# Attention in a one-layer encoder: two heads' probabilities turned in 32x32 blocks through DRAM, scores over 64 rows two heads at once, and a new order of the mixer

## The chip, the cores and the metric

One Trainium2 chip, one of its cores. The metric is the device time of one execution in microseconds (us). A core has five engines, each with its own list of instructions: TensorE (PE, matmuls; its weight loads are shown apart as PEld), VectorE (DVE), ScalarE (ACT), GpSimd (POOL) and SyncE (SP, which here only starts DMA transfers). Engines wait for each other through semaphores. PE writes to PSUM, eight banks of 128 x 512 f32; DVE and ACT read PSUM and read and write SBUF.

## The reference

One layer of an encoder on 512 positions with 1024 channels, all float32: a gated feed-forward half-step (2752 wide), a mixer, a second feed-forward half-step, a final norm. The mixer is what matters here:

```python
h = rms_norm(x, mix_norm); u = h @ w_in            # 512 Fourier | q 8x64 | k 2x64 | v 2x64
f_out = fourier_mixer(u[..., :512], fnet_w, fnet_b)
# attention, 8 query heads, 2 key heads (4 query heads share one), heads of 64:
q = rope(rms_norm(q, q_norm)); k = rope(rms_norm(k, k_norm))
scores = q @ k.T * 64**-0.5
p = softmax(scores)                                # over 512 keys
a_out = p @ v
x = x + concat([f_out, a_out]) @ w_out
```

## The kernel before, in words

Channels lie on the partitions and positions along the free axis. Products keep float32 accuracy by splitting each operand into a rounded high part and a low rest (`.h` and `.l` below, the rest by `lows`, one subtraction on DVE) and adding three of the four products: high x high, high x low, low x high.

The feed-forward halves run from the start to about 331 us and from about 485 us to the end. Neither is touched. Between them stands the mixer, written as some 660 small named operations. A string `ORDER` lists their names; `manual_schedule` emits them in that order, so that on each of the five engines the instructions stand, and run, in the order of the list. PSUM banks are handed out by `bank_for` and come back with `read`, also in list order: an operation that takes a bank waits until the last reader of the bank's former tile is done.

The attention runs over four pairs of heads, t = 0 to 3. In a pair, head b = 0 uses the first key head and b = 1 the second; their 64 channels are the lower and the upper 64 partitions. For each chunk c of 128 queries or kc of 128 keys there are these operations (t, b, c stand in the names as digits):

- `q{t}.0` to `.7`, `k.0` to `.7`, `v.0` to `.7`: projections, three matmuls a step, with weights loaded by `w...r` (SP), `.h` (ACT), `.l` (DVE). `.sq`, `.sw`, `.sd`, `.rc`, `.rs`, `.pq`, `.s0`, `.s1` are norm and rotation. `.ah`, `.al`, `.bh`, `.bl` make the stationary operands `qa` and `qb`: for head b = 0 the high part lies in one half of the partitions and the rest in the other half, and the reverse for b = 1. `k0.0` to `k1.3` build four key tiles `ks` in the same way, so that one matmul over 128 rows adds two of the products.
- `s{t}{b}{c}` (L1174, L1175): scores of 128 queries against 512 keys, two matmuls over 128 rows into one bank. `m` (L1180, L1181): the row maximum, negated and scaled, on DVE. `e` (L1188): exp on ACT, with the row sum. `g` (L1220): 1 / row sum. `n` (L1223): the probabilities scaled by it, on ACT.
- `t{t}{b}{kc}` (L1200): four transposes on PE, by which the keys come onto the partitions. `h` (L1205, ACT) and `l` (L130 into `pl`, DVE) split them, reading PSUM. `v{t}{b}{kc}` (L1234): two matmuls with the values. `o..c`, `o..a`, `r` put the two halves of the result together.
- `f..`, `map`, `d..`, `c..` are the Fourier group, and `y{d}.{k}` the output projection, eight steps for each of eight groups of channels; `y..x` and on add to x and begin the next norm.

Of the kernel before, what the change touches and what calls it, by code (L numbers as in the profile page):

```python
# [29 lines left out]
NS = 12  # L30

# [18 lines left out]
wk.r wq2.r wq0.r wq1.r wk.h wk.l wv.r k.0 k.1 wq0.h k.2 wq0.l k.3 wq1.h k.4 k.5 k.6 k.7 n1.c k.sq q0.0 cos  # L50
wq2.h q0.1 k.pq q0.2 q0.3 n1.m k.rc f0.r q0.4 q0.5 k.s0 q0.6 wq2.l k.s1 q0.7 k.sw q0.sq q2.0 wq1.l kw kp wv.h
q0.pq q1.0 k.rs q0.rc q2.1 q1.1 q1.2 q0.s0 q1.3 km q1.4 q0.sw k0.0 wv.l k1.0 q1.5 q1.6 q0.rs q0.ah q0.bh k0.3
q1.7 k0.2 k1.1 q1.sq k1.3 k0.1 q2.2 wq3.r q2.3 q1.sw q0.al q0.s1 k1.2 v.0 q0.bl q2.4 s001 s002 q1.rc s011
wq3.h m001 s010 m011 pos q2.5 s013 v.1 q1.sd q2.6 m010 e011 q2.7 e001 m002 m013 wq3.l s012 e002 s000 e010
e013 v.2 m012 f1.r q2.sq q2.sw v.3 q1.rs f0.h q3.0 v.4 e012 s003 g01 g02 v.5 f3.r m003 q1.ah q1.pq q3.1 v.6
q2.sd m000 q3.2 n002 v.7 q1.bh n001 q1.s0 n012 q1.al e000 e003 q1.s1 q1.bl f1.h s103 n1.p q3.3 g00 q3.4 g03
q2.rc vt n000 q3.5 n003 vp m103 t000 f1.l vs t003 n011 f0.l n010 q3.6 e103 n013 q3.7 t001 h000 h001 t002
q2.rs q3.sw s101 l001 v.h f00.0 l000 f2.r h002 m101 s110 q2.bh s111 l002 v.l f02.0 m111 q2.bl q3.sq f2.h o0.r
f00.1 s100 e101 f00.u m110 m100 e111 t011 g11 q3.sd s112 v000 v001 m112 h003 q2.pq h011 f02.1 l003 l011 v002
s113 s102 q2.ah q2.s0 n101 q2.s1 e100 e110 v003 t010 n111 f02.e h010 m113 t012 q2.al m102 h012 e113 e102  # L60
q3.rc o00.c t013 g13 f03.0 e112 l010 f02.h g10 f2.l f03.1 f01.0 fw.r o1.r n103 n100 v010 s213 l012 q3.pq g12
h013 o00.a q3.rs n102 f01.1 m213 f3.h f01.u q3.s0 v011 s203 v012 l013 t100 e213 fw.h m203 n110 t101 h100 h101
t102 f3.l t103 v013 l100 f10.0 o01.c q3.ah f10.1 f03.e s210 l101 h102 o01.a f03.h e203 s202 n112 l102 g23
q3.bh s212 v100 m210 n113 n203 v101 m212 h103 e210 fw.l q3.s1 m202 f12.0 t113 f02.l f12.1 r0.h l103 f10.u
q3.al s201 t110 v102 s200 v103 o4.r e212 h113 r0.l f12.e f03.l t111 t112 n213 e202 m200 f11.0 h110 o10.c l110
o10.a f13.0 m201 o2.r h111 e200 f12.h e201 g20 s211 q3.bl o0.h g22 o3.r l111 n200 m211 s303 f11.1 e211 m303
f13.1 n202 map1 f11.u v110 o1.h o5.r l113 map0 o0.l h112 f13.e f12.l d00 s313 map0.h v111 g21 l112 e303
map0.l n201 m313 map1.h s301 d01 f13.h d0.h t200 n210 d10 m301 f13.l d11 h200 n212 d1.h v112 t201 d0.l v113
map1.l c0.s l200 h201 o6.r d1.l t203 o11.c l201 t202 c0.c c0.q c1.s o11.a h203 e313 e301 h202 s312 v200 l203
c0.o c1.c m312 v201 n211 l202 s310 s311 c1.q e312 t210 g33 c0.h t213 h210 o2.h d20 d21 d2.h v202 t211 c1.o  # L70
v203 m310 e310 l210 t212 h211 c1.h d30 m311 h212 o2.l s300 n303 d2.l l211 e311 v210 l212 d31 c2.c c0.l h213
v211 m300 l213 d3.h n313 s302 m302 g31 c2.s v212 e300 c1.l v213 y0.0 y2.0 e302 g30 c2.q o21.c d3.l g32 n311
y2.1 n310 n312 c3.s o1.l c2.o c2.h n302 n300 y0.1 y1.0 c3.c o21.a t311 c3.q o7.r o20.c n301 y1.1 t310 c2.l
y0.2 y2.2 h310 y1.2 c3.o t300 c3.h o20.a t302 t301 l310 h300 c3.l l300 h302 v310 y0.3 r1.h l302 h301 h311
l301 v300 y2.3 t312 l311 v301 t303 v311 h303 t313 h312 r1.l l303 l312 v302 h313 y0.4 v303 y0.5 v312 l313 v313
r2.h y1.3 o30.c y1.4 o31.c y2.4 o30.a o31.a r2.l y1.5 y0.6 r3.h r3.l y0.7 y2.5 o5.h y0.x y0.q y1.6 y1.7 y2.6
# [12 lines left out]
def encoder(ctx, tc, A, out):  # L89
# [16 lines left out]
    tp = ctx.enter_context(tc.tile_pool(name="temps", bufs=2))  # L106
    pp = ctx.enter_context(tc.tile_pool(name="psum", bufs=8, space=bass.MemoryType.PSUM))
# [71 lines left out]
    def turned(ap):  # L179
        return ap.rearrange("p (a b c) -> p b a c", b=4, c=4)  # L180
# [598 lines left out]
    with tc.tile_pool(name="mix", bufs=1) as mp, tc.tile_pool(name="mixt", bufs=1) as mt:  # L779

        room(mp, 96)
        kst = [[mp.tile([P, S], F32R, name=f"ks{v}{o}") for o in range(2)] for v in range(2)]
# [83 lines left out]
        def rope_ops(name, g):  # L866
# [3 lines left out]
            @op(f"{name}.sq")  # L870
            def _():
                sqs[name] = mt.tile([P, S], F32, tag="sqm", bufs=3, name=f"sq_{name}")
                nc.scalar.activation(sqs[name], banks[name], AF.Square)
                read(name)
# [61 lines left out]
        def query_ops(t):  # L936
            name = f"q{t}"
            rope_ops(name, qkg[:, 0:1])

            @op(f"{name}.ah")  # L940
            def _():
                qa[t] = part[8 + t]
                nc.scalar.copy(qa[t][0:HD], rots[name][0:HD])

            @op(f"{name}.al")
            def _():
                lows(qa[t][HD:P], rots[name][0:HD], qa[t][0:HD])

            @op(f"{name}.bh")
            def _():  # L950
                qb[t] = part[12 + t]
                nc.scalar.copy(qb[t][HD:P], rots[name][HD:P])

            @op(f"{name}.bl")
            def _():
                lows(qb[t][0:HD], rots[name][HD:P], qb[t][HD:P])
# [3 lines left out]
        def key_ops():  # L960
# [20 lines left out]
            for v in range(2):  # L981
                own = slice(v * HD, (v + 1) * HD)
                oth = slice((1 - v) * HD, (2 - v) * HD)
                h1, h2 = kst[v]
                op(f"k{v}.0")(lambda own=own, h1=h1: nc.scalar.copy(h1[own], rots["k"][own]))
                op(f"k{v}.1")(lambda own=own, oth=oth, h1=h1: lows(h1[oth], rots["k"][own], h1[own]))
                op(f"k{v}.2")(lambda own=own, oth=oth, h2=h2: nc.scalar.copy(h2[oth], rots["k"][own]))
                op(f"k{v}.3")(lambda own=own, h1=h1, h2=h2: lows(h2[own], rots["k"][own], h1[own]))
# [177 lines left out]
        def score_ops(t, b, c):  # L1166
            n = f"{t}{b}{c}"
            f = sc[:, c, 2 + 2 * t + b : 3 + 2 * t + b]

            @op(f"s{n}")  # L1170
            def _():
                q = (qa, qb)[b][t][:, c * P : (c + 1) * P]
# [395 lines left out]
```

## Time and profile before

| | |
|---|---|
| three runs, median (lowest to highest) | 819.46 us (818.97 to 819.93) |
| the profiled execution: its time, its span | 818.9 us, 817.1 us |
| granted TensorE clock | 0.998 |
| mixer: first projection to last output step | 330.9 to 485.0 us |

The span goes from the first to the last instruction. The busy time of an engine counts its own instructions; the releaser of a wait is what ended it. A group's mean is the length of one record; where records overlap, as on PE, what counts is the distance from one start to the next.

### The profile page before, as it was taken

How to read it: one execution, taken by the hardware profiler on the slowest of the kernel's cores; microseconds unless marked ns; L12 is line 12 of the kernel's file. 1: busy time of each engine (PE TensorE's matmuls, PEld its weight loads, DVE VectorE, ACT ScalarE, POOL GpSimd, SP SyncE). 2: the span in 40 equal slices, each digit the busy share in tenths (PEclk: the TensorE clock that was granted, in tenths of full speed). 3: DMA queues.
4: the chain of work that ended last, by engine and by line, in shares of the span. 5: the costliest groups of instructions: out<-in, count | busy, mean ns of one | idle time of the engine just before them, and what ended most of it. 6: DMA issues, size and time to landing. Idle time of an engine off the chain costs nothing.

```text
span 817.1 us, 13011 instructions
## 1 busy us (share of the span) xinstructions
PE 810.0 (99%) x4936; PEld 729.1 (89%) x4936; DVE 652.0 (80%) x1080; ACT 503.5 (62%) x871; POOL 67.7 (8%) x75
## 2 busy tenths in 40 slices
PE   9999999999999999999999999999999999999997
PEld 7888998899989998889998888899988998899987
DVE  7997997489856867799998588999955997489674
ACT  7883774167623735689999449557733674267462
POOL 0320000000000000221000003100100000000001
PEclk9999999999999999999999999999999999999999
DMA  7874553345343423342101236564443553345223
GB/s 258 198 176 167 150 130 91 123 130 168 85 138 94 130 71 117 130 149 65 66 26 52 79 101 145 128 188 143 134 116 111 153 144 79 134 130 145 60 78 103
DMA packets 37534, 99.75 MB, mean 122 GB/s; under 512 B 4448, under 2 KB 10720, under 8 KB 37472
## 3 DMA queue, kind: packets, MB, share of 16 engines
q1 hardware_dynamic: 27776, 82.61, 31.4%
q0 software_dynamic: 8832, 15.34, 11.0%
q10 hardware_dynamic: 864, 0.98, 0.3%
q8 instruction: 38, 0.62, 0.3%
q14 instruction: 24, 0.20, 0.1%
HBM read 93.41 MB, written 2.10 MB: 117 GB/s over the span
## 4 chain that ended last, share of the span: by engine, by line
PE 96%; DMA 1%; DVE 1%; ACT 1%; issue 0%; POOL 0%; POOLq 0%; DVEq 0%; ACTq 0%
PE dn L186 24%; PE r L436 12%; PE mix L186 8%; PE r L441 8%; PE gu L186 8%; PE q L436 4%; PE q L441 4%; PE r L432 4%; PE p L432 4%; PE q L432 4%; PE gu L740 3%; PE p L441 2%; PE mix L1234 2%; PE mix L1200 2%; PE mix L1038 1%; PE mix L1039 1%
## 5 line engine op out<-in xcount | busy, mean ns | idle before, releaser
L186 PE MATMUL dn<-at,ring 128*128 128x512 f32 x900 | 202.8, 380 | 0.8 <-DVE ring L130 0.8
L186 PEld LDWEIGHTS dn<-at,ring 128*128 128x128 f32 x900 | 167.9, 188 | 29.8 <-DVE ring L130 1.2
L441 PE MATMUL r<-rt,ring 128*128 128x256 f32 x560 | 154.3, 276 | 0.0
L436 PE MATMUL r<-rt,ring 128*128 128x256 f32 x840 | 147.1, 276 | 0.0
L436 PEld LDWEIGHTS r<-rt,ring 128*128 128x128 f32 x840 | 127.1, 188 | 1.6
L441 PEld LDWEIGHTS r<-rt,ring 128*128 128x128 f32 x560 | 105.1, 188 | 0.2
L391 ACT CAST ring<-s 128x1024 fp32r<-128x1024 f32 x70 | 73.6, 1051 | 35.6 <-PE r L436 16.5
L130 DVE TENSOR_TENSOR ring<-s,ring 128x1024 fp32r<-128x1024 f32 x70 | 85.2, 1217 | 12.1 <-ACT ring L391 10.1
L575 DVE SCALAR_TENSOR_TENSOR gx<-dn,gx 128x512 f32<-128x512 f32 x61 | 41.8, 688 | 61.9 <-PE dn L186 61.8
L172 ACT CAST ring<-raw_dn 128x768 fp32r<-128x768 f32 (+3 forms) x58 | 45.3, 783 | 70.6 <-PE dn L186 55.8
L441 PE MATMUL q<-rt,ring 128*128 128x256 f32 x280 | 77.0, 275 | 0.0
L160 POOL DMA_DIRECT2D ring<-in_wgu x38 | 32.9, 866 | 470.9 <-ACT u L450 372.8
L130 DVE TENSOR_TENSOR ring<-raw_dn,ring 128x768 fp32r<-128x768 f32 (+3 forms) x58 | 51.5, 891 | 9.0 <-ACT ring L172 4.9
L441 PEld LDWEIGHTS q<-rt,ring 128*128 128x128 f32 x280 | 52.6, 188 | 0.0
L130 DVE TENSOR_TENSOR ring<-raw_g,ring 128x1024 fp32r<-128x1024 f32 x35 | 42.7, 1219 | 9.8 <-PE p L432 9.5
L436 PE MATMUL q<-rt,ring 128*128 128x256 f32 x280 | 49.8, 277 | 0.0
L186 PE MATMUL gu<-ring 128*128 128x512 f32 x216 | 48.9, 381 | 0.0
L432 PE MATMUL r<-rt,ring 128*128 128x512 f32 x140 | 48.5, 383 | 0.0
L432 PE MATMUL q<-rt,ring 128*128 128x512 f32 x140 | 48.4, 382 | 0.0
L432 PE MATMUL p<-rt,ring 128*128 128x512 f32 x140 | 48.3, 382 | 0.0
L186 PEld LDWEIGHTS gu<-ring 128*128 128x128 f32 x216 | 40.4, 188 | 6.9
L391 ACT CAST ring<-raw_g 128x1024 fp32r<-128x1024 f32 x35 | 36.8, 1051 | 13.6 <-DMA raw_g<-in_wgu 10.6
(277 smaller groups left out, 1658.6 us busy)
## 6 DMA issues: line engine op xcount, KB each, us to landing
raw_g<-in_wgu SPq DMA_DIRECT2D x35, 512.0 KB, 3.8
raw_u<-in_wgu SPq DMA_DIRECT2D x35, 512.0 KB, 4.5
raw_dn<-in_wd SPq DMA_DIRECT2D x40, 384.0 KB, 3.2
ring<-in_wgu POOLq DMA_DIRECT2D x35, 256.0 KB, 4.3
raw_gu<-in_wgu SPq DMA_DIRECT2D x12, 512.0 KB, 3.9
raw_o<-in_wo SPq DMA_DIRECT2D x8, 512.0 KB, 3.3
raw_dn<-in_wd SPq DMA_DIRECT2D x8, 448.0 KB, 3.3
raw_wq<-in_wins SPq DMA_DIRECT2D x4, 512.0 KB, 3.4
```

The costliest lines, as they stand in the source:

```text
L130: nc.vector.tensor_tensor(out=lo, in0=src, in1=asf(hi), op=ALU.subtract)
L160: nc.gpsimd.dma_start(out=lo, in_=src, accum_op=ALU.add)
L172: nc.scalar.copy(hi[:, :n, :], raw[:, :n, :])
L186: nc.tensor.matmul(ps, a, b, start=first and b is mhi and a is whi, stop=last and a is wlo)
L391: nc.scalar.copy(hi, src)
L432: nc.tensor.matmul(turned(ps), whi[:, ks], turned(m), start=start, stop=False, skip_group_check=True)
L436: nc.tensor.matmul(ps[:, t], whi[:, ks], m[:, o * HALF :][:, t], start=start and o == 0, stop=False, skip_group_check=True,)
L441: nc.tensor.matmul(o, wlo[:, ks], m, start=False, stop=stop, skip_group_check=True)
L575: nc.vector.scalar_tensor_tensor(out=x[d][:, t], in0=ps[:, t], scalar=0.5, in1=x[d][:, t], op0=ALU.mult, op1=ALU.add)
L740: nc.tensor.matmul(turned(pss[c]), w[:, k % 2, c], turned(m[k]), start=k == 0 and m is hh and w is hi, stop=k == KD - 1 and w is lo,)
L1200: nc.tensor.transpose(pts[n][:, c * P : (c + 1) * P], prob[t, b, c][:, kc * P : (kc + 1) * P], ident)
L1234: nc.tensor.matmul(turned(outs[t, b]), w, turned(p), start=kc == 0 and i == 0, stop=kc == 3 and i == 1)
```

## The change

1. **Scores.** The keys are kept once as a high and a low tile (`k.h`, `k.l`, one instruction each on ACT and DVE over all 128 partitions, where `k0.0` to `k1.3` were four and four over 64), and so is a pair's query (`q{t}.h`, `q{t}.l` for `.ah`, `.al`, `.bh`, `.bl`). `s{t}{c}` makes both heads of a pair: six matmuls with a contraction over 64 rows, alternately on partitions 0 to 63 (head 0, one bank) and 64 to 127 (head 1, another bank). `m{t}{c}` has two reductions and one multiplication of two columns.
2. **Two heads' probabilities** (t = 0, b = 0 and 1). Their `t` operations, 32 transposes on PE, are gone. The exp writes its 512 columns in 32-column blocks; after scaling, DVE turns 128 x 512 elements in 32x32 blocks in place (`T`, four a head); SP writes each to DRAM (`Z`, 256 KB, four a head) and reads it back with rows of blocks on other partitions (`z`, four a head). `h` and `l` then read SBUF.
3. **Buffers.** The probabilities of a head are one tile, two such tiles in turn (before: nine tiles of one chunk in turn). The reserve for descriptors of POOL's DMAs goes from 16384 to 8192 bytes a partition.
4. **Order.** The whole list is another one.

```diff
+BY_BLOCKS = "00", "01"
+REST_BY_DMA = {'00': (), '01': ()}
 ORDER = """
-wk.r wq2.r wq0.r wq1.r wk.h wk.l wv.r k.0 k.1 wq0.h k.2 wq0.l k.3 wq1.h k.4 k.5 k.6 k.7 n1.c k.sq q0.0 cos
+wq1.r wq0.r wk.r cos wk.h wk.l wq2.r k.0 k.1 wv.r wq0.h wq3.r k.2 k.3 k.4 k.5 k.6 wq0.l k.7 n1.c k.sq wq1.h n1.m q0.0
...
-            @op(f"{name}.ah")
+            @op(f"{name}.h")
             def _():
                 qa[t] = part[8 + t]
-                nc.scalar.copy(qa[t][0:HD], rots[name][0:HD])
...
+                nc.scalar.copy(qa[t], rots[name])
...
+                lows(qb[t], rots[name], qa[t])
...
+            op("k.h")(lambda: nc.scalar.copy(kst[0], rots["k"]))
+            op("k.l")(lambda: lows(kst[1], rots["k"], kst[0]))
...
+                @op(f"T{t}{b}{g}")
+                def _(g=g):
+                    nc.vector.transpose(heads[t, b][:, g], heads[t, b][:, g])
...
+                    nc.sync.dma_start(out=outside[t, b][g], in_=heads[t, b][:, g])
...
+                        moved[t, b] = mt.tile([P, 4, S], F32, tag="pt", bufs=2, name=f"pt{t}{b}")
+                    source = outside[t, b][g].rearrange("(a i) f -> i a f", a=4)
+                    nc.sync.dma_start(out=moved[t, b][g * 32 : (g + 1) * 32], in_=source)
...
+                nc.scalar.copy(natural(ph), source())
...
-                nc.tensor.matmul(turned(sps[n]), q, turned(kst[b][0]), start=True, stop=False)
-                nc.tensor.matmul(turned(sps[n]), q, turned(kst[b][1]), start=False, stop=True)
+                for i, (w, m) in enumerate(((qa[t], kst[0]), (qa[t], kst[1]), (qb[t], kst[0]))):
+                    for b in range(2):
+                        r = slice(b * HD, (b + 1) * HD)
+                        nc.tensor.matmul(
+                            turned(sps[n][b]), w[r, cs], turned(m[r]), start=i == 0, stop=i == 2,
+                            skip_group_check=True,
+                        )
...
+                for b in range(2):
+                    nc.vector.tensor_reduce(out=mx[:, b : b + 1], in_=sps[n][b], axis=AX.X, op=ALU.max, negate=True)
...
+    nc = bacc.Bacc("TRN2", target_bir_lowering=False, num_devices=1, dynamic_dma_scratch_size=8192)
```

On PE, at the first scores, before. `mix` with a number is a PSUM bank's tile, `ks` a key tile, `near` the tile with the queries, `ring` and `more` weights:

```order
L186 MATMUL mix_3292<-ring 128x4x32x4 x3
L1174 MATMUL mix_3291<-ks_3275,near 128x4x32x4
L1175 MATMUL mix_3291<-ks_3276,near 128x4x32x4
L1174 MATMUL mix_3288<-ks_3275,near 128x4x32x4
L1175 MATMUL mix_3288<-ks_3276,near 128x4x32x4
L1174 MATMUL mix_3294<-ks_3277,near 128x4x32x4
L1175 MATMUL mix_3294<-ks_3278,near 128x4x32x4
L1174 MATMUL mix_3293<-ks_3277,near 128x4x32x4
L1175 MATMUL mix_3293<-ks_3278,near 128x4x32x4
L186 MATMUL mix_3292<-ring 128x4x32x4 x3
```

The same place now, from the last two matmuls of the second chunk on (the chunk before it wrote `mix_3289` and `mix_3291` in six such rows; L917 is `q1.pq`):

```order
L1217 MATMUL mix_3288<-ks_3277,near 128x4x32x4
L1217 MATMUL mix_3292<-ks_3277,near 128x4x32x4
L1217 MATMUL mix_3294<-ks_3277,near 128x4x32x4
L1217 MATMUL mix_3290<-ks_3277,near 128x4x32x4
L1217 MATMUL mix_3294<-ks_3278,near 128x4x32x4
L1217 MATMUL mix_3290<-ks_3278,near 128x4x32x4
L1217 MATMUL mix_3294<-ks_3277,near 128x4x32x4
L1217 MATMUL mix_3290<-ks_3277,near 128x4x32x4
L185 MATMUL mix_3295<-ring 128x4x32x4 x3
L185 MATMUL mix_3293<-ring 128x4x32x4 x3
L917 MATMUL mix_3291<-ident,sq_q_3469 128x128 x4
L185 MATMUL mix_3295<-ring 128x4x32x4 x6
```

Eighteen score matmuls stand in a row, alternating between two banks; after them come two projection steps, and then four transposes that take over bank `mix_3291`, which the first chunk's second head has filled.

On DVE at the same place, before (`mx` is the maximum, `rot` the rotated query):

```order
L130 TENSOR_TENSOR ring<-raw_wv,ring 128x1024
L909 TENSOR_TENSOR sw_q_3432<-sw_q_3432,sin 128x512
L910 TENSOR_TENSOR rot_q_3412<-rot_q_3412,sw_q_3432 128x512
L130 TENSOR_TENSOR ks_3276<-rot_k,ks_3275 64x512
L130 TENSOR_TENSOR ks_3277<-rot_k,ks_3277 64x512
L130 TENSOR_TENSOR ks_3278<-rot_k,ks_3277 64x512
L130 TENSOR_TENSOR ks_3275<-rot_k,ks_3275 64x512
L130 TENSOR_TENSOR near<-rot_q_3412,near 64x512 x2
L901 TENSOR_TENSOR rot_q_3485<-own_q_3469,cos 128x512
L1180 TENSOR_REDUCE mx_3490<-mix_3291 128x1
L1181 TENSOR_TENSOR mx_3490<-mx_3490,sc 128x1
```

And now:

```order
L129 TENSOR_TENSOR ks_3278<-rot_k,ks_3277 128x512
L129 TENSOR_TENSOR near<-rot_q_3436,near 128x512
L129 TENSOR_TENSOR ring<-raw_wv,ring 128x1024
L1226 TENSOR_REDUCE mx_3471<-mix_3289 128x1
L1226 TENSOR_REDUCE mx_3471<-mix_3291 128x1
L1227 TENSOR_TENSOR mx_3471<-mx_3471,sc 128x2
L1226 TENSOR_REDUCE mx_3475<-mix_3288 128x1
L1226 TENSOR_REDUCE mx_3475<-mix_3292 128x1
L1227 TENSOR_TENSOR mx_3475<-mx_3475,sc 128x2
```

The query's low part, for which the first scores wait, is now directly ahead of the value weights' low part and the first two maxima.

On SP, before (`raw_f` and `raw_fw` are weights of the Fourier group, `sw_q` the swap of a query's halves):

```order
L154 DMA raw_f_3368<-in_winf 128x1024
L154 DMA raw_wq_3463<-in_wins 128x1024
L895 DMA sw_q_3468<-own_q_3469 32x512 x4
L154 DMA raw_f_3550<-in_winf 128x1024
L154 DMA raw_f_3578<-in_winf 128x1024
L895 DMA sw_q_3554<-own_q_3555 32x512 x4
L154 DMA raw_f_3707<-in_winf 128x1024
L154 DMA raw_o_3741<-in_wo 128x1024
```

And now (`th` is a head's probabilities, `out` its place in DRAM, `pt` the tile that is read back):

```order
L153 DMA raw_f_3545<-in_winf 128x1024
L1162 DMA out_3588<-th_3501 128x512 x3
L1162 DMA out_3628<-th_3498 128x512 x3
L1162 DMA out_3588<-th_3501 128x512
L1162 DMA out_3628<-th_3498 128x512
L153 DMA raw_fw<-in_fw 128x512
L1169 DMA pt_3667<-out_3628 32x4x512 x2
L891 DMA sw_q_3646<-own_q_3647 32x512 x4
L1169 DMA pt_3667<-out_3628 32x4x512
L1169 DMA pt_3710<-out_3588 32x4x512
L1169 DMA pt_3667<-out_3628 32x4x512
```

Eight writes and the reads stand in SP's list between the weights and the swaps; a read waits for its own write.

More of the change, by code (lines that the diff above doesn't have):

```diff
@@ L55 @@
[L55 to L64, printed above, removed]
```

154 lines of the change are left out of this document (95 added, 59 removed).

## The prediction

> **What bounds the kernel now.** I read the page's parts 1 and 4 first.
>
> ```profile
> span 817.1 us, 13011 instructions
> PE 810.0 (99%) x4936; PEld 729.1 (89%) x4936; DVE 652.0 (80%) x1080; ACT 503.5 (62%) x871; POOL 67.7 (8%) x75
> PE 96%; DMA 1%; DVE 1%; ACT 1%; issue 0%; POOL 0%; POOLq 0%; DVEq 0%; ACTq 0%
> ```
>
> PE is busy for 99% of the span and holds 96% of the chain that ended last: over the whole, PE's work is the time. The mixer has to be read for itself, so I cut it into windows (columns: the window, its length; busy us and instructions of each engine; granted clock; DMA share; GB/s).
>
> ```profile
> core 0: us, PE busy (x) PEld busy (x) DVE busy (x) ACT busy (x) POOL busy (x), PEclk, DMA share, GB/s
> 345.00:365.00 20.00, 20.00 (x93) 16.92 (x92) 18.34 (x38) 17.90 (x33) 3.29 (x4) 1.00 0.50 157
> 365.00:385.00 20.00, 19.95 (x136) 17.90 (x135) 19.46 (x39) 18.71 (x38) 5.30 (x3) 1.00 0.23 70
> 385.00:405.00 20.00, 20.00 (x151) 18.85 (x150) 19.31 (x41) 19.76 (x40) 1.64 (x1) 1.00 0.20 67
> 405.00:425.00 20.00, 20.00 (x141) 18.53 (x140) 19.09 (x41) 19.29 (x39) 0.00 (x0) 1.00 0.08 27
> 425.00:445.00 20.00, 20.00 (x124) 17.77 (x124) 18.24 (x39) 19.75 (x40) 0.00 (x0) 1.00 0.17 53
> 445.00:465.00 20.00, 20.00 (x98) 17.03 (x97) 12.82 (x17) 10.51 (x16) 0.00 (x0) 1.00 0.20 63
> ```
>
> From 345 to 445 us, the attention, three engines are full at once: PE 99.95 us of 100, DVE 94.4 (18.34 + 19.46 + 19.31 + 19.09 + 18.24), ACT 95.4. From 445 on DVE and ACT have room. So a us off PE is a us off the time only as far as DVE and ACT follow.
>
> **PE: what is removed and added.** The rows of PE, first by line (count, busy us, mean ns), then three pieces of the chain (start, us, what) and three records in order of time.
>
> ```profile
> L1200 PE MATMUL mix<-ident,e 128*128 128x128 f32 x128 | 17.2, 272 | 0.0
> L1174 PE MATMUL mix<-ks,near 128*128 128x512 f32 x32 | 12.6, 394 | 0.1
> L1175 PE MATMUL mix<-ks,near 128*128 128x512 f32 x32 | 12.3, 384 | 0.0
> 368.81 0.87 PE mix L1200 x8
> 369.69 1.36 PE mix L186 x6
> 451.30 8.82 PE mix L186 x40
> 352.73 0.40 PE L1174 MATMUL mix<-ks,near 128*128 128x512 f32 x1
> 352.73 0.19 PEld L1175 LDWEIGHTS mix<-ks,near 128*128 128x128 f32 x1
> 352.97 0.38 PE L1175 MATMUL mix<-ks,near 128*128 128x512 f32 x1
> ```
>
> In the chain a 512-column matmul takes 8.82 / 40 = 0.22 us of PE and a transpose 0.87 / 8 = 0.109, while their records read 0.38 and 0.27: the records overlap, so I price by the chain.
>
> - *Transposes*: 32 of the 128 go: 32 x 0.109 = 3.5 us less. They carry their own weight loads away with them.
> - *Scores*: 64 matmuls (14.1 us) become 96 over 64 rows. No row of this trace is a matmul over less than 128 rows (every form reads 128*128), so this price is bounded. Below, two heads run side by side and a pair costs one 512-column pass: 48 x 0.22 = 10.6, a gain of 3.5. Above, each costs a pass: 96 x 0.22 = 21.1, a loss of 7.0. Their loads are no end beyond these: eight transposes, each with a load of its own, follow at 0.109, and six loads at that pace are 0.65 us against 0.66 for three passes. I take the lower end, because the two heads use different rows of the array and different banks and nothing of the one needs the other.
> - *Changing between 128 and 64 rows*: the scores stand in 11 separate runs, so 22 changes. Nearest row: from transposes to products the next six matmuls took 1.36 us where six take 1.32, or 0.04 lost. The upper end is a pipeline that empties, 0.38 - 0.22 = 0.16 a change. I take 22 x 0.025 = 0.5; ends 0 and 3.5.
>
> [...] No run shown here has such a change. [...]
>
> **DVE and ACT.** The rows by line (x, busy us, mean ns), all within the mixer:
>
> ```profile
> L1180 DVE TENSOR_REDUCE mx<-mix 128x1 f32<-128x512 f32 x32 | 21.8, 682 | 0.0
> L1181 DVE TENSOR_TENSOR mx<-mx,sc 128x1 f32<-128x1 f32 x32 | 5.1, 159 | 1.4
> L130 DVE TENSOR_TENSOR near<-rot_q,near 64x512 fp32r<-64x512 f32 x8 | 5.5, 686 | 0.2
> L130 DVE TENSOR_TENSOR ks<-rot_k,ks 64x512 fp32r<-64x512 f32 x4 | 2.7, 684 | 0.0
> L965 DVE TENSOR_SCALAR kw<-sc 128x512 f32<-128x512 f32 x1 | 0.4, 428 | 0.4 <-POOL sc L932 0.4
> L130 DVE TENSOR_TENSOR ring<-raw_wv,ring 128x1024 fp32r<-128x1024 f32 x1 | 1.2, 1215 | 0.0
> L1188 ACT ACTIVATE e<-mix,mx,sc 128x512 f32<-128x512 f32 x32 | 25.0, 786 | 0.0
> L1205 ACT CAST ph<-mix 128x512 fp32r<-128x512 f32 x32 | 18.4, 595 | 2.8 <-PE mix L1200 2.2 <-PE mix L1234 0.3
> L943 ACT CAST near<-rot_q 64x512 fp32r<-64x512 f32 x4 | 2.5, 623 | 0.2 <-DVE rot_q L910 0.2
> L985 ACT CAST ks<-rot_k 64x512 fp32r<-64x512 f32 x2 | 1.2, 618 | 0.0
> ```
>
> - *DVE*: four query rests and three key rests fewer, 7 x 0.685 = 4.8 us less (64 partitions cost what 128 do); 16 small multiplications fewer, 16 x 0.159 = 2.5 less; the reductions stay 32. Added: 8 block transposes of 128 x 512. None is in the trace; the rows of that size go from 0.43 (`kw`) to 0.69, and I take 0.68, since most of them lie there: 5.4 us. Net 1.9 less (ends 1.8 and 3.9).
> - *ACT*: four query and three key copies fewer, 7 x 0.62 = 4.3 us less. The eight `h` that now read SBUF in blocks go from 0.595 to some 0.62, 0.2 more; I price the blocked exp and scaling as before. Net 4.1 less.
> - *What this makes of PE's 7.0*: if all of it came off the stretch of 100 us, DVE would have 94.4 - 1.9 = 92.5 us of work in 93.0. The fullest DVE window above is 19.46 of 20, 97.3%; at that share 92.5 needs 95.1 us. ACT at its fullest, 98.8%, needs 91.3 / 0.988 = 92.4 and does not bind. So 2.1 us of PE's gain turn into waits for DVE, by list position after 400 us, where scores, maxima and low parts stand thick. With block transposes at 0.43 this term is 0.
>
> **The first exps.** Bank `mix_3291` of the first chunk's second head is taken over by the transposes of `q1.pq`, after 18 score matmuls and two projection steps. Until then DVE has to do the value weights' low part and the first maxima, and ACT its table load, which in this trace stands waiting ahead of the first exp:
>
> ```profile
> 355.30 1.28 ACT L1188 ACT_TABLE_LOAD   x1 [1.64 <-DVE mx L1181]
> PEld mix L1174 <- DVE near L130: 0.5, 1, 0.5
> ```
>
> From the moment the query's rest is done: 1.22 + 2 x 0.68 + 0.16 + 1.28 + 0.79 = 4.8 us to the end of the exp. PE has 9 x 0.22 for three chunks of scores and 6 x 0.22 for the steps, 3.3 us. PE waits 1.5. The second row is the one like wait of the order before. If a pair costs two passes PE has 5.3 us and the wait is 0.
>
> **The way through DRAM.** SP issues 16 more transfers. The nearest rows (KB, us to landing; then SP's longest wait):
>
> ```profile
> raw_fw<-in_fw SPq DMA_DIRECT2D x1, 256.0 KB, 2.7
> SPq L895 <- ACT own_q L881: 10.4, 2, 8.0
> ```
>
> From the last block transpose to the first `v01`: issue, write and read at 2.7 each, `h` 0.6, `l` 0.7, about 7 us, and 3 to 4 more for eight reads in one queue at some 0.4 an issue. Between them PE has, in the new list, seven half projections of the Fourier group (12 matmuls each, at no less than the 0.109 of a load: 9.2 us), two chunks of scores (1.3), five projection steps (3.3) and eight transposes (0.9): 14.7 us. That hides it with 4 us over; if that cover goes, each us late is a us on PE. Queued behind the reads on SP are a swap of a query's halves and the weights `o0` and `f3`. SP has already stood 8.0 us at a swap without PE waiting. DVE's turns, ACT's wait for a buffer until the write has landed (the exps of pair 1) and POOL's smaller reserve (75 instructions, 8% busy) lie beside work; I cost them at nothing, 0 to 2 us. The tail, from 445 us on, keeps its PE work, with DVE at 64% and ACT at 53%; nothing there.
>
> **Sum.** -3.5 - 3.5 + 0.5 + 2.1 + 1.5 = -2.9 us against the profiled execution's own 818.9, or 816.0. That execution lies 0.56 under the median of the runs, 819.46; on the median the forecast is 816.5. For the likeliest case alone, by the ends of the changes (0 to 3.5), the DVE term (0 to 3) and the first exps (0.5 to 2): 814 to 818.6.
>
> **The rivals.**
>
> - *The heads don't run side by side (slower).* The 96 matmuls queue: +7.0 in place of -3.5. PE is then 3.5 us above before, the waits for DVE and the first exps vanish, and with 0 to 3.5 for the changes the time is 823 to 826.5, middle 824. For it: no two matmuls of this trace run at once, they start 0.22 us apart whatever the bank. Against it: all of them use all 128 rows, so they could not. It decides from a price of about 0.35 us a pair, where 48 pairs cost 6 us more than I took.
> - *The full gain.* Block transposes at 0.43 and enough lead on DVE: -7.0 + 0.5, no waits: 813. For it, DVE does 5% less than PE in the stretch today; against it, its windows are full just where the list is thick.
> - *Gain given back (no change).* A weight load that can't go beside a pass on the same rows makes 0.11 + 0.22 for each, 0.99 a chunk: scores 15.8 us, 1.7 more than before; with the transposes' 3.5 and 1 us of waits the time is 818.7. The trace speaks against it: the load at 352.73 runs under the matmul at 352.73 on the same rows. The same time comes out if SP's chain or the two-tile buffer makes PE wait 2 us. [...]
> - *Read-back late.* Weights held up behind a read on SP, or `v01` early: +3 to +5 on the sum, 820 to 822.
>
> **How the numbers follow.** Likeliest case 0.50, not side by side 0.22, full gain 0.11, given back 0.12, late 0.05. 0.2% is 1.6 us, about what a measurement of this kernel tells from no change: faster is under 817.8, slower over 821.1. Of the likeliest four fifths are faster, the rest the same; the full gain is faster; given back is the same but for a quarter on either side; late is slower by half; not side by side is slower. Faster 0.40 + 0.11 + 0.02 = 0.53; same 0.10 + 0.07 + 0.02 = 0.19; slower 0.22 + 0.03 + 0.03 = 0.28. The range, 812.3 to 824.8, leaves out the lower part of the full gain (0.03), and the upper third or so of the first rival (0.08).
>
> **What would show it.** Right: the two score matmuls of a pair start about 0.11 us apart and pairs follow at 0.22; the gap behind the last pair is under 0.1; PE idles some 1.5 us ahead of `q1.pq` with ACT's exp as releaser and some 2 us ahead of `v` or `y` steps after 400 us with DVE as releaser; block transposes read about 0.68; no PE wait ends on the read-back. Wrong: score matmuls 0.22 apart each, a wait ahead of the first `v01` or behind the weights `f3`, or DVE windows under 90% while PE waits.

## The result, and the profile after

| | us | ratio to before, 95% interval |
|---|---|---|
| before, median of 4 runs beside it | 819.35 (818.97 to 819.93) | |
| changed kernel, median of 4 runs | 825.57 (824.02 to 827.54) | 1.0077, 1.0054 to 1.0099 |

The change made the kernel 6.2 us slower, where 3 us faster was forecast. The profiled execution took 825.55 us. The parts of its page that answer to those shown of before:

```profile
span 823.8 us, 13012 instructions
PE 811.9 (99%) x4936; PEld 723.8 (88%) x4936; DVE 649.3 (79%) x1065; ACT 499.7 (61%) x864; POOL 67.1 (8%) x75
PE 87%; ACT 5%; DVE 4%; DMA 2%; issue 1%; POOL 0%; SPq 0%; POOLq 0%; DVEq 0%; ACTq 0%
```

PE still reads 99% busy, but it holds 87% of the chain instead of 96%; ACT, DVE and DMA have taken the rest. By windows:

```profile
core 0: us, PE busy (x) PEld busy (x) DVE busy (x) ACT busy (x) POOL busy (x), PEclk, DMA share, GB/s
345.00:365.00 20.00, 18.81 (x96) 14.73 (x95) 17.17 (x35) 18.12 (x34) 5.93 (x6) 1.00 0.44 146
365.00:385.00 20.00, 19.74 (x142) 17.05 (x140) 17.34 (x30) 11.89 (x26) 0.00 (x0) 1.00 0.96 253
385.00:405.00 20.00, 18.03 (x110) 16.26 (x109) 16.16 (x32) 16.60 (x31) 3.76 (x2) 0.83 0.24 70
405.00:425.00 20.00, 20.00 (x145) 16.52 (x143) 18.34 (x39) 18.79 (x40) 0.00 (x0) 1.00 0.09 27
425.00:445.00 20.00, 19.54 (x118) 15.28 (x117) 18.83 (x40) 19.84 (x41) 0.00 (x0) 1.00 0.20 59
445.00:465.00 20.00, 20.00 (x108) 17.04 (x108) 13.05 (x21) 13.67 (x23) 0.00 (x0) 1.00 0.05 21
```

Three things are new. In 365 to 385 us the DMA engines are full (0.96, before 0.23) and ACT has 11.89 us of work instead of 18.71. In 385 to 405 PE halts and its granted clock falls to 0.83. And 445 to 465 has 13.67 us of ACT's work, 3 more than before: work that came late.

What PE waited for in the mixer (who waited for whom, us in total, times, longest):

```profile
PE mix L1290 <- ACT ph L1183: 1.9, 1, 1.9
PE mix L917 <- ACT th L1243: 1.2, 1, 1.2
PE mix L1256 <- ACT th L1279: 0.5, 1, 0.5
PE mix L1290 <- DVE near L129: 0.3, 1, 0.3
```

L1290 are the attended products, L1183 the copies `h` of what was read back, L917 `q1.pq`. The transfers of that stage (KB, median us from issue to landing, so with the time in the queue), and then the last block transpose on DVE and ACT at the copies (start, length, wait ahead and its releaser):

```profile
out<-th SPq DMA_DIRECT2D x8, 256.0 KB, 2.2
pt<-out SPq DMA_DIRECT2D x8, 256.0 KB, 5.6
```

```profile
368.41 0.70 DVE L1156 STREAM_TRANSPOSE th<-th 128x512 f32<-128x512 f32 x1
381.39 1.14 ACT L1183 CAST ph<-pt 128x512 fp32r<-128x512 f32 x2 [3.00 <-DMA pt<-out]
387.30 0.62 ACT L1183 CAST ph<-pt 128x512 fp32r<-128x512 f32 x1 [1.45 <-issue]
```

The same 256 KB take 2.2 us to DRAM and 5.6 us back. By the transfer records the reads landed mostly 1.2 to 1.4 us apart, the last at 387.24. The view names no releaser for ACT's second wait (`issue`), but `h000`, which needs that last read, begins 0.06 us behind it, at 387.30. PE from there (start, length):

```profile
387.98 0.79 PE L1290 MATMUL mix<-ph,near 128*128 128x512 f32 x1 [1.86 <-ACT ph L1183]
...
389.29 0.41 PE L1020 MATMUL mix<-more,ring 128*128 128x256 f32 x1
389.51 0.41 PE L1021 MATMUL mix<-more,ring 128*128 128x256 f32 x1
...
394.76 0.28 PE L1020 MATMUL mix<-more,ring 128*128 128x256 f32 x1
394.87 0.28 PE L1021 MATMUL mix<-more,ring 128*128 128x256 f32 x1
```

The wait of 1.86 us stands ahead of `v000`. After it matmuls of 256 columns start 0.21 us apart instead of 0.11, up to 394.2 us. And the parts whose price was in doubt, by line (x, busy us, mean ns), then by PE records:

```profile
L1217 PE MATMUL mix<-ks,near 64*128 64x512 f32 x96 | 13.5, 403 | 0.0
L1156 DVE STREAM_TRANSPOSE th<-th 128x512 f32<-128x512 f32 x8 | 5.1, 684 | 0.2 <-ACT th L1279 0.2
```

```profile
349.67 2.28 PE L1217 MATMUL mix<-ks,near 64*128 64x512 f32 x18
351.88 0.50 PE L185 MATMUL mix<-ring 128*128 128x512 f32 x1
355.42 1.28 PE L185 MATMUL mix<-ring 128*128 128x512 f32 x5
356.63 0.94 PE L1217 MATMUL mix<-ks,near 64*128 64x512 f32 x6
357.50 1.16 PE L185 MATMUL mix<-ring 128*128 128x512 f32 x4
```

Eighteen score matmuls take 351.88 - 349.67 = 2.21 us, 0.123 each: two heads do run side by side (a pass each would be 3.96). The single chunk takes 357.50 - 356.63 = 0.87, where three passes are 0.66, and the five matmuls before it 1.21 instead of 1.10: 0.32 us for the two changes, so the change of rows cost on both of its sides. To see where PE lost time, take for every matmul of the mixer the distance to the next start, less the pace of its kind (0.218 us for 512 columns, 0.112 for 256, 0.109 for a transpose). The sum is 3.6 us before and about 16.2 after. Of the 12.6 more, 3.3 stand at the changes of rows, 1.4 ahead of `q1.pq` (1.2 of it idle), 3.7 at the first attended products, 2.3 in the stretch at half pace, and 1.9 in many small waits. Of these only one is long enough for the views to name its releaser, 0.5 us behind ACT at 444 us. The 7.0 us are the work that the change took off PE, 3.5 for the transposes and 3.5 for the pairs; 12.6 - 7.0 = 5.6 is what the mixer grew by (153.97 to 159.62).

### The profile page after: what moved, and what is told of

The parts are those of the page before. It is cut to its first block, busy times and chain, and to the rows that moved or that the text cites. A ratio compares the mean times of both kernels' runs of the same rounds, so it can differ in the third digit from the quotient of the medians.

```text
span 823.8 us, 13012 instructions
## 1 busy us (share of the span) xinstructions
PE 811.9 (99%) x4936; PEld 723.8 (88%) x4936; DVE 649.3 (79%) x1065; ACT 499.7 (61%) x864; POOL 67.1 (8%) x75
## 4 chain that ended last, share of the span: by engine, by line
PE 87%; ACT 5%; DVE 4%; DMA 2%; issue 1%; POOL 0%; SPq 0%; POOLq 0%; DVEq 0%; ACTq 0%
PE dn L185 24%; PE r L435 12%; PE r L440 8%; PE gu L185 7%; PE mix L185 6%; PE q L435 4%; PE q L440 4%; PE r L431 4%; PE p L431 4%; PE q L431 4%; PE gu L739 3%; ACT th L1243 2%; PE p L440 2%; PE mix L1290 1%; ACT th L1279 1%
## 5 line engine op out<-in xcount | busy, mean ns | idle before, releaser
L129 DVE TENSOR_TENSOR ring<-s,ring 128x1024 fp32r<-128x1024 f32 x70 | 85.3, 1218 | 12.3 <-ACT ring L390 10.2
L129 DVE TENSOR_TENSOR ring<-raw_dn,ring 128x768 fp32r<-128x768 f32 (+3 forms) x58 | 51.5, 891 | 9.2 <-ACT ring L171 4.8
L129 DVE TENSOR_TENSOR ring<-raw_g,ring 128x1024 fp32r<-128x1024 f32 x35 | 42.7, 1220 | 9.9 <-PE p L431 9.6
```

The costliest lines, as they stand in the source:

```text
L129: nc.vector.tensor_tensor(out=lo, in0=src, in1=asf(hi), op=ALU.subtract)
```

## The experiments

Times are medians against before on the same chip, 5 rounds each (e8: 3); the median of before lay between 819.1 and 819.6 throughout. Differences of two experiments below about 1 us are not told apart. Scores are other numbers in e2, e4 and e13, and rows stand in another order in e11, e12 and e13: these price a part and are no kernels to use.

**e1, turns back on PE**, put into the list ahead of their copies.

```diff
-BY_BLOCKS = "00", "01"
+BY_BLOCKS = ()
-heads[t, b] = mt.tile([P, 4, S], F32, tag="th", bufs=2, ...)
+heads[t, b] = mt.tile([P, 4, S], F32, tag="th", bufs=4, ...)
-... T000 ... Z000 ... z011 ... s12 f00.1 h011 ... h010 ... l010 ...
+... t010 s12 t011 f00.1 h010 l010 ... h011 l011 ...
```

> The changed kernel with the block way of heads 00 and 01 undone: their 8 turns are transposes on PE again (32 matmuls more), the 8 block transposes and 16 transfers are gone, scores stay in pairs over 64 rows. Theory (the read-back came late, and PE's halt lowered its clock): 3.3 us of waits and 2.5 us of half pace go, 3.5 us of transposes come back: 823.3 us, between 821.5 and 824.5, and the clock stays at 1.00 through 385 to 395. Rival (the new order itself is slow, and the waits would be somewhere in any case): PE only gets 3.5 us more to do, 827 to 829.

825.56 us (1.0078, 1.0064 to 1.0092), outside both ranges; the clock was not lowered, as the theory said. The changed kernel took 825.57, so the block way as built saves nothing: its 3.5 us less of PE are paid back by the read-back. That e1 was not faster still lay in the list written for it, where PE waited 2.0 us for a bank (PE L1256 on DVE pl L129).

**e5, the same with the turns spread.**

```diff
-... q2.s0 n100 f01.u n112 q3.rs f3.h n102 t012 v002 t100 n111 h012 l012 f3.l n113 t003 f10.1 ...
+... q2.s0 f01.u q3.rs t012 h012 l012 v002 t003 h003 l003 n100 n102 q3.s0 t013 h013 l013 f03.e v012 f3.h f10.0 f3.l ...
```

> As e1 (turns of heads 00 and 01 on PE), with another order of the same operations between 380 and 400 us: f10.0, n10x, n11x and f3's parts stand behind the turns, so that the turns don't share one PSUM bank. e1's trace shows PE 2.3 us in wait there (0.7 and 1.6, for DVE's low parts), which are of its order and not of the change. Theory (read-back and lowered clock cost 5.8 in the changed kernel, turns 3.5): 825.6 - 2.3 = 823.3, between 822.5 and 824.3. Rival (DVE and ACT end late whatever PE does before 405, so e1 and the changed kernel end alike by them): 825 to 826, with the waits moved behind 405 us.

824.54 us (1.0062, 1.005 to 1.0074), 1.2 more than the theory's middle and between the two ranges: this list has a wait of its own, 1.1 us for `f3`'s low part (PE L1022 on DVE ring L129).

**e2, scores over 128 rows**, with blocks as changed.

```diff
-for i, (w, m) in enumerate(((qa[t], kst[0]), (qa[t], kst[1]), (qb[t], kst[0]))): ... w[r, cs], turned(m[r])
+for i, (w, m) in enumerate(((qa[t], kst[0]), (qb[t], kst[1]))): ... w[:, cs], turned(m)
```

> The changed kernel with each score chunk as 4 matmuls over 128 rows in place of 6 over 64 (both heads' rows are summed, so the scores are other numbers; 64 passes in place of 48, and no change between 128 and 64 rows). Theory (a change costs 0.21 us, 20 of them 4.2, and eats the pairs' gain of 3.5): 0.7 us faster than the changed kernel, 824.9 us, between 824 and 825.8. Rival (the price on record, 0.5 us for all the changes): 3.0 us slower, 828.5. Second rival (pairs gain nothing): 7 us faster, 818.

824.29 us (1.0059, 1.0047 to 1.0072), 1.3 faster than the changed kernel and in the theory's range. This is no clean price of the pairs, though: in e2's trace the clock stays up at the read-back.

```profile
385.00:405.00 20.00, 18.56 (x128) 16.42 (x129) 18.77 (x36) 18.58 (x35) 4.15 (x2) 1.00 0.22 67
```

The half pace that is missing there was worth 2.3 us of PE in the changed trace, so the 1.3 us may be the clock's. e13 prices the pairs against a kernel whose clock stays up as well.

**e4, neither**: the edits of e1 and e2 together.

> Both undone in the changed order: turns of 00 and 01 on PE, scores over 128 rows (summed over both heads, so other numbers). What is left of the change is the order and the fewer copies of queries and keys. Theory (order costs the 1.4 us ahead of the first turned squares and about as much again in small waits): 822.6 us, between 821 and 824, which is e1 less 0.7. Rival (the order is what costs): 825 or more. Rival (the order is harmless): 819 to 820.

826.29 us (1.0083, 1.0069 to 1.0097), in the range of the rival by which the order is what costs. Its trace has e1's bank wait (2.0 us, PE L1252 on DVE pl L129), so it can't price the order alone; with that taken off it would be 824, the theory's upper end. That is argued, not shown.

**e8, twenty half-row matmuls** among the output steps.

```diff
+def half_rows():
+    nc.tensor.matmul(turned(spare[0]), kst[0][0:HD, 0:P], turned(kst[0][0:HD]), start=True, stop=True)
```

> The changed kernel with 20 matmuls of 512 columns over 64 rows added in the last stage of the mixer, each between two 128-row matmuls of the output projection (y5.0 to y4.3), where PE waits for nothing: 20 passes and 40 changes between 128 and 64 rows. Theory (0.21 us a change): 20 x 0.22 + 40 x 0.21 = 12.8 us more than the changed kernel, 838.4, between 837 and 839.5. Rival (the price on record, 0.025 a change): 5.4 more, 831. Rival (a pipeline that empties, 0.16): 10.8 more, 836.4.

839.11 us (1.0241, 1.0225 to 1.0257), 13.5 more than the changed kernel, in the theory's range: (13.5 - 20 x 0.22) / 40 = 0.23 us a change. PE there:

```profile
467.73 0.48 PE L1395 MATMUL mix<-ks 64*128 64x512 f32 x1
468.14 0.94 PE L186 MATMUL mix<-near,ring 128*128 128x512 f32 x3
469.01 0.49 PE L1395 MATMUL mix<-ks 64*128 64x512 f32 x1
```

Three products and one half pass, 0.88 us of passes, take 469.01 - 467.73 = 1.28: 0.20 for each change. This is the price shown by itself, with a weight load at each change. In the changed trace the 20 changes cost 3.3 / 20, some 0.16 each.

**e6, PE kept busy** ahead of the waits.

```diff
+def fill(n):
+    for _ in range(n): nc.tensor.matmul(turned(spare[0]), kst[0][:, 0:P], turned(kst[0]), start=True, stop=True)
-... v010 ... v000 ...
+... x0 v010 ... x1 v000 ...
```

> The changed kernel with idle work on PE ahead of the waits for the read-back: 3 passes of 512 columns ahead of v010 and 10 ahead of v000 (2.9 us, into a free bank, read by no one). Theory (PE's halt of 2 us at 386 us is what lowers the clock from 388 to 394): matmuls stay at 0.11 us, 2.2 us go, 823.4, between 822.8 and 824.5; waits end at the same times. Rival (the clock falls for another reason, as the load of the DMA engines): 825 to 826, half pace stays. Rival (the passes come in the way): 826 to 828.

```profile
385.00:405.00 20.00, 19.68 (x136) 16.94 (x136) 17.94 (x36) 18.29 (x34) 4.14 (x2) 1.00 0.27 71
```

824.66 us (1.0068, 1.0051 to 1.0086). With idle passes in the halt the clock stays at 1.00 (0.83 in the changed kernel) and the mixer is 1.35 us shorter; the lowered clock comes from the halt. Of the 2.2 us forecast only 0.9 reached the medians, within what two experiments can't tell apart. In the changed trace the clock falls at 387.3 us:

```profile
383.90:387.30 3.40, 1.84 (x10) 1.00 (x8) 2.50 (x5) 1.96 (x5) 0.00 (x0) 1.00 1.03 263
387.30:394.20 6.90, 6.22 (x26) 5.69 (x27) 6.17 (x13) 6.90 (x12) 1.96 (x1) 0.51 0.12 29
```

In the 3.4 us ahead of the fall PE was busy for 1.84, and that did not keep the clock up.

**e7, reads first** in SP's queue.

```diff
-Z013 ... fw.r ... z011 ... z010 ... q2.sd ... z012 ... z003 ... z013 ... z002 ... o0.r ... z000 z001
+Z013 z010 z011 z012 z013 z000 z002 z003 z001 ... fw.r ... q2.sd ... o0.r
```

> The changed kernel with all 8 reads ahead in SP's queue of fw, the swap of q2 and o0 (head 01's four first), and q2's rest, high and low parts later on DVE and ACT. Theory (the last two reads stood behind the swap, o0 and 4 us of issue): the last read lands by 383.5 instead of 387.2, PE's wait ahead of v000 falls from 2.0 to under 0.5 us, the clock stays up: 820.5 us, between 819.5 and 822.5. Rival (the DMA engines bring 256 KB each 1.27 us whatever the order): the last read lands at 385 or later, 823.5 to 825. Rival (the order is wrong elsewhere, and ACT and DVE end late in any case): reads early, but 824.5 to 826.

826.62 us (1.0086, 1.0072 to 1.01), slower than all three said. The last read landed at 382.52, as the theory had it, but the swap behind the reads landed later (its last part at 384.34 instead of 377.51), and ACT's next copy of a query waits for its buffer:

```profile
384.41 0.69 ACT L877 ACTIVATE own_q<-mix,qkg 128x512 f32<-128x512 f32 x1 [6.33 <-DMA sw_q<-own_q]
```

```profile
PE mix L1020 <- ACT own_q L877: 2.3, 1, 2.3
```

With the DMA engines full (0.96 in 365 to 385 us of e7), this order only chose who was late.

**e9, later use** of what is read back, and **e10**, in addition `q1.pq` later.

```diff
-... h011 g13 f02.0 h010 ... e110 v.h ... q2.rs v.l l010 ... e102 h000 ... v010 q3.pq ... v000 ... f12.0 ... f03.1 ... v011 f10.0 ...
+... f00.u e110 v.h ... q2.rs f02.e v.l ... e102 h010 h011 h000 q2.l q3.pq ... l010 l000 ... f12.0 f03.1 ... f10.0 ... v010 v000 v011 ...
-... q1.pq g00 q2.2 q1.s0 q2.3 e002 pos s03 v.1 g02 q2.4 ...                       # e10
+... q2.2 q2.3 e002 g00 pos v.1 g02 q2.4 s03 q1.sd v.2 e011 q1.pq v.3 ... m03 q1.s0 ...
```

> The changed kernel with the same work, in another order around the read-back: ACT does e110, v.h, e112, e102 and n10x ahead of the copies h010, h011, h000 that wait for it; DVE does q2's rest, f02.e, q2.l ahead of l010; PE does the half projections f12.0, f03.1, f10.0 (4.1 us) ahead of the first attended products v010, v000, v011. Theory (the read-back's 3.7 us of waits and 2.3 us of half pace are paid only because the products stood too early): PE waits under 0.5 us there, clock at 1.00, 825.6 - 6 = 819.6, between 818.8 and 821.5. Rival (DVE and ACT end late behind 405 us whatever stands before): 823 to 825, with new PE waits for DVE's low parts behind 400 us.

> e9, and the turned squares q1.pq four projection steps later (behind s03, v.2), so that PE has 2.6 us of steps while ACT works through the first exps. Theory: the wait of 1.4 us ahead of q1.pq goes and nothing takes its place, 1.3 us less than e9: 818.3, between 817.3 and 820.2. Rival (the exps' lateness comes out at s03 or at q3.0, or DVE's later sums delay what follows): within 0.5 us of e9.

e9 823.55 us (1.0058, 1.0045 to 1.0071), e10 826.27 (1.0085, 1.0071 to 1.0099): 2 us of the 6 in e9, none in e10. The 2 us go with the clock: e9's runs took 823.37 to 823.55 us at a mean granted clock of 0.999 or 1.0, but 825.25 at 0.998 and 826.25 at 0.995, and e10's lay at 0.995 to 0.997. In e9 ACT stood behind the same read:

```profile
388.77 0.62 ACT L1183 CAST ph<-pt 128x512 fp32r<-128x512 f32 x1 [4.71 <-DMA pt<-out]
```

Its copies and scalings then came in a heap, and PE waited 1.4 us for one of the copies among the attended products. In e10 the wait went from `q1.pq` to DVE's weights (PE L1022 on DVE ring L129, 1.4 us).

**e3, one read a head**, with DRAM in the order of the read.

```diff
+outside[t, b] = dp.tile([4, 32, 4, S], ...)
+nc.sync.dma_start(out=outside[t, b][g].rearrange("i a f -> a i f"), in_=heads[t, b][:, g])
+nc.sync.dma_start(out=moved[t, b], in_=outside[t, b].rearrange("g i a f -> (g i) a f"))      # once a head
```

> The changed kernel, with the blocks laid out in DRAM in the order in which they are read, and one read of 1 MB over 128 partitions for each head, at the place of the last of the four, in place of four of 256 KB over 32. Theory (late because four slow reads onto 32 partitions and their turns in SP's queue): the read lands within 5 us of the last write, no PE wait ends on the first attended products, the clock stays up: 3.3 + 2.5 us go, 819.8, between 818.5 and 821.5. Rival (the DMA engines are full with 4 MB there and back in any form, or DVE's turns end too late): at most 2 us go, 823.5 to 825.5.

```profile
DMA  0213121222222222222222222222222296975873
GB/s 25 41 8 16 33 57 74 102 94 107 98 106 98 102 102 102 102 98 106 102 102 98 106 102 102 98 107 102 102 98 102 102 168 262 303 143 127 176 197 131
```

833.73 us (1.018, 1.0166 to 1.0194), slower than both said. The reads were fast (382 to 448 GB/s in 390.5 to 395 us), but the writes now went at about 102 GB/s, with a DMA share of 0.2 (40 slices of 364 to 384 us, share in tenths); ACT waited 17.6 us for them to free `th`, and PE 12.6 for ACT. Why the writes in this order were slow is not shown.

**e11, rows of 8 KB**, and **e12, one read of 1 MB onto 128 partitions**; writes as in the changed kernel.

```diff
-source = outside[t, b][g].rearrange("(a i) f -> i a f", a=4)
+source = outside[t, b][g].rearrange("(i a) f -> i a f", a=4)              # e11
+source = outside[t, b].rearrange("g (i a) f -> (g i) a f", a=4)           # e12, once a head, into moved[t, b]
```

> The changed kernel, whose reads back take the same 256 KB of DRAM as 32 rows of 8 KB (one for each partition) in place of 128 rows of 2 KB: the rows come in another order, so the probabilities stand wrong, all else is as it was. In the changed kernel the reads land 1.2 to 1.3 us apart, the writes 0.6 to 0.7. Theory (short rows make the reads slow, and the late read-back holds ACT's queue, PE and then the clock): reads land 0.6 to 0.8 us apart, the last by 383, PE's waits there under 1 us, clock at 1.00: 825.6 - 5 = 820.6, between 819.5 and 822. Rival (32 partitions make them slow): 1.2 us apart as before, 825 to 826. Rival (ACT and DVE are late behind 405 us in any case): reads early, 823.5 to 825.

> The changed kernel, whose read back is one transfer of 1 MB for each head, 128 rows of 8 KB onto 128 partitions, at the place of the last of the four (rows in another order, as in e11; the writes as in the changed kernel, not as in e3). e3's reads of this kind moved 390 to 450 GB/s. Theory (the reads alone are at fault): 1 MB in 2.5 us, the second read issued at 377 and landed by 381.5, 820, between 819 and 821.5. Rival (the wait for SP's turn and for DVE's last block turns sets it): landed no earlier than 384, 823 to 825. Rival as in e11 (late in any case): 823.5 to 825.

e11 826.48 us (1.0086, 1.0072 to 1.01), near the rival of the 32 partitions; e12 819.45 (1.0002, 0.9993 to 1.0011), in the theory's range. Windows while the reads run, of the changed kernel, e11 and e12, each from its own answer (last two columns DMA share, GB/s):

```profile
375.40:380.40 5.00, 5.00 (x43) 4.48 (x42) 4.95 (x9) 2.99 (x7) 0.00 (x0) 1.00 1.06 208
```

```profile
375.40:380.40 5.00, 5.00 (x42) 4.48 (x42) 4.95 (x9) 3.20 (x7) 0.00 (x0) 1.00 1.04 212
```

```profile
374.00:381.00 7.00, 7.00 (x61) 6.48 (x60) 6.92 (x13) 6.91 (x16) 0.00 (x0) 1.00 0.96 370
385.00:405.00 20.00, 20.00 (x153) 17.96 (x153) 19.41 (x35) 18.55 (x36) 4.14 (x2) 1.00 0.09 28
```

In these windows the full engines moved 208 GB/s onto 32 partitions, with short rows (212 with long ones), and 370 onto 128. With one read a head onto 128 partitions, the waits at the read-back and the half pace are gone (PE 20.00 and clock 1.00 in 385 to 405), and 6.1 us with them. PE's waits that are left in e12's mixer:

```profile
PE mix L917 <- ACT th L1245: 1.2, 1, 1.2
PE mix L1258 <- ACT th L1281: 0.4, 1, 0.4
```

e12 also has two reads instead of eight. What speaks against this as the cause are the writes: eight of 256 KB each, they landed mostly 0.6 to 0.7 us apart from 128 partitions, and 1.09 from 32 in e14 below. Why the transfers over 32 partitions were slower is not shown.

**e13, e12 with e2's scores**: both edits together.

> e12 (one read of 1 MB for each head, rows in another order) with the score chunks of e2 (4 matmuls over 128 rows, both heads summed): the price of the pairs, where the read-back no longer stands over it. Theory (20 changes at 0.17 to 0.23 us, 3.4 to 4.6, against 3.5 saved by the pairs; 0.4 less wait ahead of the first turned squares): 0.3 to 1.5 us faster than e12, 818.6, between 817.9 and 819.4. Rival (the price on record, 0.5 for all changes): 2.6 slower, 822. Rival (DVE sets the pace in that stage, not PE): as e12, 819.2 to 819.8, and smaller waits take the place of the changes.

820.16 us (1.0012, 1.0003 to 1.0021): 0.7 slower than e12, and the intervals overlap. No theory's range held it. By the mixers of the two traces the pairs are worth 0.5 us (153.51 with them, 154.01 without), by the two intervals between nothing and some 2 us, changes included; not the 3.0 of the forecast.

**e14, writes from 32 partitions, one read of 128**, rows in their own order.

```diff
+into = outside[t, b].rearrange("g i a f -> a i g f")[a]
+nc.sync.dma_start(out=into, in_=heads[t, b][a * 32 : (a + 1) * 32])       # four a head, after its last T
```

> The changed kernel with right values and e12's kind of read: each head is written by four transfers from 32 partitions (all four blocks of a row at once), after its last block transpose, into DRAM rows in the order of the read, and read by one transfer of 1 MB onto 128 partitions. Theory A (it is the writing of SBUF 32 partitions at a time that is slow, reading it is not): writes land 0.6 to 0.8 us apart, the last read by 382, near e12: 820, between 819 and 821.5. Theory B (a transfer that touches only 32 partitions takes 1.25 us for 256 KB in either direction): writes 1.2 to 1.3 apart, the last read at 385 to 387, 823 to 825.5.

826.62 us (1.0092, 1.0078 to 1.0106), above both ranges. The eight writes landed between 372.15 and 379.78, 1.09 apart: slow in this direction too, as theory B said. The time lies above theory B's, since `th` stays taken longer: ACT's exps of the next pair wait 9.8 us for the writes, and PE 2.4 and 1.9 us for ACT's exps.

**e15, reads of blocks 2 and 3 from ACT's queue**, rows in their own order and these reads earlier in the list, and **e16**, `q1.pq` later as well.

```diff
-nc.sync.dma_start(out=moved[t, b][g * 32 : (g + 1) * 32], in_=source)
+(nc.sync if g < 2 else nc.scalar).dma_start(out=moved[t, b][g * 32 : (g + 1) * 32], in_=source)
-... Z001 e101 Z013 ... z011 ... z010 ... z012 ... z003 ... z013 ... z002 ... z000 z001 ...
+... Z001 z002 z003 e101 Z013 ... z012 z013 z011 ... z010 ... z000 z001 ...
-... q1.pq g00 q2.2 q1.s0 q2.3 e002 pos s03 v.1 ...                                # e16
+... g00 q2.2 q2.3 e002 pos v.1 s03 q1.pq g02 ... m03 q1.s0 ...
```

> The changed kernel with right values: the reads onto partitions 64 to 127 (blocks 2 and 3 of each head) are issued from ACT's queue, those onto partitions 0 to 63 from SP's as before, so that a read of either half can run beside one of the other. [...] Rival (the 16 DMA engines take transfers one after the other, whatever the queue): reads 1.2 us apart as before, 824.5 to 826. Rival (four issues and their waits on ACT cost more than they bring): over 826.

> e15, and the turned squares q1.pq three projection steps and one score chunk later (behind v.1 and s03, which stays ahead of them), q1.s0 behind m03 on DVE. Theory: the wait of 1.4 us ahead of q1.pq falls under 0.4 and nothing takes its place: 1 us less than e15. Rival (as in e10, DVE or ACT give it back later): within 0.5 us of e15 or slower.

e15 822.95 us (1.0043, 1.0027 to 1.0059), e16 822.7 (1.0039, 1.0025 to 1.0053). For two reads at a time 821.5 was on record, between 820 and 823. e15's time lies in that range, but not for that reason: no two reads landed less than 1.07 us apart, the last at 386.32. What is different is that two reads were issued from 367.15 on instead of 370.68, and that the clock stayed at 1.00; that the 2.6 us come from these two is argued, not shown. In e16 the wait of 1.2 us left `q1.pq`, but PE now waited 1.1 us for DVE's weights; a wait of 1.0 ahead of `vp` stood in e15 too (1.1). No version found here beats the kernel before.

## Why the prediction was wrong, point by point

The step that failed first is the way through DRAM, put at nothing; the second is the price of the changes between 128 and 64 rows. The measured 825.57 us falls into the 823 to 826.5 of the rival "the heads don't run side by side", but that is chance: its mechanism didn't occur.

- *Transposes*, 3.5 us off PE: no trace shows it apart, but the sum below closes with it.
- *Two heads side by side*: right, 0.123 us a matmul. The rival with the largest chance fell.
- *Changes between 128 and 64 rows*: failed, by its size. 0.025 us each was taken, with 0.16 as the upper end; the changed trace has 0.16, e8 0.20 to 0.23. There are 10 runs of scores and 20 changes, not 11 and 22, and they cost 3.3 us by the trace, nearly all of the pairs' 3.5. The nearest row, transposes to products, had no change of rows in it, so its 0.04 said nothing. The upper end given for all of them, 3.5, is about right.
- *DVE too full*, 2.1: the small waits in the changed trace are 1.9. The size fits, the cause is not shown: the one that the views name, at 444 us, ends on ACT. In e12, where the read-back doesn't hold it, DVE has 92.15 us of work in 345 to 445, where 92.5 were reckoned.
- *First exps*, 1.5: measured 1.4, with ACT's exp as releaser, as the text said.
- *Block transposes*, 0.68 each: 0.684.
- *The way through DRAM*, costed at nothing: this step failed, and it decides that the kernel became slower. The price of a read was taken from `raw_fw`, which has the same 256 KB but 128 partitions; onto 32 a read kept the engines for 1.25 us (256 KB at 208 GB/s). Eight of them and the transfers between made 18 us from the end of the last block transpose (369.1) to the last landing (387.24), where 10 to 11 were reckoned with the copies behind it, against 14.7 us of cover up to the first `v01`. The long wait came behind that, at `v000`, whose tile was read last. Beyond PE's 3.7 us of waits the text foresaw neither that ACT, in its order, stands behind the copies (its work then comes late) nor that PE's halt lowers the clock (0.51 for 6.8 us). Together 6.1 us by e12. The rival "read-back late" came nearest to the mechanism, but at +3 to +5, 820 to 822, and with a chance of 0.05.
- *The range*: the ends given for the terms of the likeliest case add up to 812.9 and 820.9, not to 814 and 818.6. The measured time lies above both; no end was given for the read-back.

The sum closes on e12. With the changed trace's terms it is -3.5 - 3.5 + 3.3 + 1.9 + 1.4 = -0.4, and e12's mixer is 153.51 us against 153.97 before. The forecast's -2.9 differs from it mainly by the changes; the changed kernel differs from e12 by the read-back. So the changes take back nearly all of the pairs' gain, the waits (1.9 + 1.4) nearly all of the transposes', and the read-back's 6.1 us stand on top.

Open: what the new order costs by itself, since each list that undid a part brought waits of its own; which engine the small waits are due to; and how much of e6's higher clock reaches the end, since its runs lie between 823.35 and 828.27 us.

## What to carry to other kernels

Price a transfer from a row with the same partitions, not only the same bytes (256 KB landed 1.2 to 1.4 us apart onto 32 partitions here, 0.6 to 0.7 from 128), and look at the DMA share of the stage in which it lands: here the way round through DRAM met engines that were full (0.96 in 365 to 385 us). Count the changes between 64 and 128 rows: two heads over 64 rows pay only when a run of scores saves clearly more than the 0.3 to 0.4 us that going there and back costs here. A wait on a read-back can cost more than itself: here, beside PE's 3.7 us of waits, the in-order queue behind it came late, and the halted PE went on at half pace (clock 0.51), which cost 2.3 us.

## What the hardware showed unexpectedly

- Transfers of 256 KB onto or from 32 partitions landed mostly 1.0 to 1.4 us apart (changed kernel, e14, e15), from 128 partitions 0.6 to 0.7; 208 GB/s onto 32 (changed kernel) against 370 onto 128 (e12) with the engines full.
- e3's writes, into DRAM in the order of the read, ran at 102 GB/s and a DMA share of 0.2.
- A change between matmuls over 128 and over 64 rows cost 0.16 us in the changed kernel and 0.20 to 0.23 in e8, each way.
- PE's clock fell to half (0.51) after 3.4 us in which PE was busy for 1.84, and stayed there for 6.8 us; with idle matmuls in the waits (e6) it read 1.00. In the other traces with a fall in the mixer it lasted 3.4 us (e7, e8 and e9, where 385 to 405 us read 0.91, and e14, 0.94 and 0.98 in 365 to 385 and 385 to 405), 6.8 (e10 and e11, 0.83) or 13.7 (e3, 0.82 and 0.83).
